# A two-layer hybrid network on one core: the last four slabs by token tile, single accumulator banks, and cross attention's loads in steps

## The chip, the core and the metric

The kernel runs on one core of a Trainium2 chip. The metric is the device time of one execution in microseconds. An engine here is one of TensorE (PE; its weight loads are PEld), VectorE (DVE), ScalarE (ACT), GpSimd (POOL) and SyncE (SP, which issues most of the DMAs).

## The reference

256 tokens of width 2048 go through two layers. Each layer adds to the residual stream h, in this order, a mixer, a cross attention over 256 memory rows, and a feed-forward network with a convolution of width 3:

```
for l in range(DEPTH):
    hn = _rmsnorm(h, norm_mix[l])
    h = h + (_mixer_ab if l % 2 == 0 else _mixer_c)(hn, ...)
    h = h + _cross_attn(_rmsnorm(h, norm_cross[l]), mem_n, w_q_x[l], w_kv_x[l], w_o_x[l])
    h = h + _conv_ffn(_rmsnorm(h, norm_ffn[l]), w_up[l], conv_w[l], conv_b[l], w_down[l])
return _rmsnorm(h, norm_final)
```

The first mixer holds eight heads of block attention and eight of compressed, selected and window attention; the second is a retention. Cross attention has four heads of 128. All is float32, and the weights (525 MB read) are used once.

## The kernel before

Every float32 product is made of three products of rounded parts: a value is split into a high part and a low rest, and high by high, high by low and low by high are summed. `weights` (L224) loads a raw weight tile of 512 KB through SP's queue into one of four buffers; ScalarE rounds it into a high tile (L231), VectorE subtracts for the low one (L232). There are two product forms. `product_b` (L257) gives features by tokens: the weight stands still and 512 columns move (both parts of 256 tokens, L271), then 256 columns (L276). `product_a` (L294) gives tokens by features: a slab of 128 inputs is held for one of two token tiles t of 128, and three matmuls (L304 to L306) run over up to 512 weight columns. A product's accumulator (`acc_tile`, L98) is one PSUM tile of two banks, of which there are two; four more single banks serve everything else.

The order of TensorE's work is written by hand. Side work (the sums of a row norm, heads of attention, the compression of keys and values, turning the residual into the next input) sits in generators in a queue, and `pump(n)` takes n steps of them between product steps. The order on ScalarE, VectorE, GpSimd and SP is a scheduler's, except in the first part.

The start: while the first product runs, rows of x are loaded for the norm's sums (`load_rows`), squared on ScalarE with a running sum (L147), and turned into 1/rms by small VectorE operations (L152 to L185). The first `product_a` after that has weight columns from 4864; its eviction multiplies by the 1/rms.

Cross attention (L528 to L582): the q products of two blocks of columns run interleaved; memory slabs come in four loads of four slabs into raw tiles (`mem_part`, L501) among the q weights; then k and v, then a head's softmax and its product with v (L570), which needs v as evicted by L577.

The feed-forward network (L850 to L897) works in chunks of hidden slabs of 128: 6, 6, 8, 8, 8, 8. While one chunk is computed upward, the one before goes downward in `out_product` (L591), four groups g of 512 columns, each followed by `residual` (L586), which adds the accumulator to h. In the last layer the last downward product is followed per g and t by a square with sum (L147) and a multiplication by the gain (L1047); at the end `norm.column` makes both tiles' 1/rms with Newton steps on VectorE, and scalings (L1055 on VectorE, L1057 on ScalarE) and eight output DMAs (L1058) close the kernel.

Of the kernel before, what the change touches and what calls it, by code (L numbers as in the profile page):

```python
# [20 lines left out]
P = 128  # L21
S = 256
# [7 lines left out]
FFN_CHUNKS = (6, 6, 8, 8, 8, 8)  # L30
# [45 lines left out]
def hybrid_kernel(ctx: ExitStack, tc: tile.TileContext, a, out):  # L76
# [21 lines left out]
    def acc_tile():  # L98
        count[0] += 1
        return ps.tile([P, 2, 512], F32, name=f"acc{count[0]}", tag="acc", bufs=2)  # L100
# [156 lines left out]
    def product_b_steps(ws, xs, evac, step=4, n=None, turn=True):  # L257
# [4 lines left out]
        for i, k0 in enumerate(range(0, n, step)):  # L262
# [6 lines left out]
            def upper(order, end):  # L269
                for k, j in order:  # L270
                    pe.matmul(acc[:, j, :], parts[k - k0][0][:, j * P : (j + 1) * P], xs[k], start=(k == 0),  # L271
                              stop=(end and k == n - 1))

            def lower(order, end):
                for k, j in order:
                    pe.matmul(acc[:, j, 0:S], parts[k - k0][1][:, j * P : (j + 1) * P], xs[k][:, 0:S], start=False,  # L276
# [10 lines left out]
        for j in range(2):  # L287
            evac(j, acc[:, j, :])
# [5 lines left out]
    def product_a_steps(w, xs, c0, ncol, evac, s0=0, ws=None, n=None):  # L294
# [3 lines left out]
        for k in range(n):  # L298
            hi, lo = next(ws)
            for t in range(2):  # L300
                o = acc[:, t, 0:ncol]
                xh = xs[k][:, t * P : (t + 1) * P]
                xl = xs[k][:, S + t * P : S + (t + 1) * P]
                pe.matmul(o, xh, hi, start=(k == 0), stop=False)  # L304
                pe.matmul(o, xh, lo, start=False, stop=False)  # L305
                pe.matmul(o, xl, hi, start=False, stop=(k == n - 1))  # L306
            if k % 2 and k < n - 1:
                yield
        for t in range(2):
            evac(t, acc[:, t, 0:ncol])  # L310
# [55 lines left out]
    with tc.manual_schedule(engines=engines):  # L366
        act.activation(new([P, 1]), eps, AF.Copy, scale=eps)
        load_par(nc.sync, "mix")
        for p in range(ND // 2):
# [14 lines left out]
            if p in (4, 6):  # L384
                for g in range(2):
                    load_rows(p // 2 - 2, g)
# [141 lines left out]
    def cross(l, xs, norm, head_done):  # L528
# [19 lines left out]
        run(*[product_b_steps(weights(w_q, 0, ND, 2 * P * blk, 2 * P), xs, ev_q) for blk in range(2)], n=4)  # L548
# [7 lines left out]
        def head(h):  # L556
# [39 lines left out]
    def mixer_ab(xs, row, col, kcv):  # L596
# [548 lines left out]
```

## Time and profile before

| quantity | us |
|---|---|
| median of 3 runs | 2854.06 (2853.86 to 2856.67) |
| the profiled execution's own time | 2853.46 |
| its span | 2851.70 |
| TensorE busy | 2818.40 |
| VectorE busy | 1923.39 |
| ScalarE busy | 1461.83 |
| first matmul starts | 6.01 |
| last matmul starts | 2836.77 |

The profile is of one execution; the span is the time from its first to its last recorded event, and the execution's own time is 1.76 us longer. The order of groups in the page is by cost; a wait is put down to the instruction that released it last.

### The profile page before, as it was taken

To read this page: it belongs to the slowest core of one execution; us is meant where nothing else is said; L and a number is where in the kernel's file an instruction comes from. 1 tells how busy PE (TensorE), PEld (TensorE's weight loads), DVE (VectorE), ACT (ScalarE), POOL (GpSimd) and SP (SyncE) were. 2 spreads that over 40 slices of the span, in tenths; PEclk is the share of its full clock that TensorE was granted. 3 is DMA by queue.
4 is the path that set the end of the run, shared out by engine and by line. 5 is a ranking of instruction groups with operands and counts; after the bars stand their busy time and mean duration, and the time that the engine had idled before them with its cause. 6 is when DMAs were issued, how large, how long until landed. Compare 5 with 4: busy or idle time off the path is not lost.

```text
span 2851.7 us, 39531 instructions
## 1 busy us (share of the span) xinstructions
PE 2818.4 (99%) x14726; PEld 2404.8 (84%) x14726; DVE 1923.4 (67%) x3139; ACT 1461.8 (51%) x2184; POOL 29.8 (1%) x211
## 2 busy tenths in 40 slices
PE   8999999999999999999999999999999999999997
PEld 7888888888888888888888888888888888888886
DVE  7766776776777677665555555565767776767675
ACT  5444455654555555454444444444565555545453
POOL 0000000000000000000000000000000000000000
PEclk9999999999999999999999999999999999999999
DMA  8534565555555555555555555555545555555554
GB/s 306 168 121 138 173 211 192 173 187 191 188 192 192 189 192 203 192 184 177 177 178 184 187 180 185 180 192 187 195 165 192 192 188 189 190 191 190 190 192 140
DMA packets 149392, 530.11 MB, mean 186 GB/s; under 512 B 16912, under 2 KB 17328, under 8 KB 149200
## 3 DMA queue, kind: packets, MB, share of 16 engines
q1 hardware_dynamic: 147600, 523.65, 53.4%
q0 software_dynamic: 1024, 2.90, 0.3%
q8 instruction: 115, 1.88, 0.3%
q10 hardware_dynamic: 576, 1.05, 0.1%
q14 instruction: 77, 0.63, 0.1%
HBM read 525.43 MB, written 2.10 MB: 185 GB/s over the span
## 4 chain that ended last, share of the span: by engine, by line
PE 96%; ACT 1%; DMA 1%; DVE 1%; issue 0%; SPq 0%; ACTq 0%; DVEq 0%
PE acc L271 32%; PE acc L276 16%; PE acc L304 15%; PE acc L306 14%; PE acc L305 14%; PE bank L338 1%; DMA t<-in_w_in_ab_dram 1%; PE bank L958 0%; ACT t L196 0%; PE bank L474 0%; PE bank L494 0%; PE bank L486 0%; DVE t L232 0%; DMA t<-in_w_kv_x_dram 0%; ACT t L231 0%
## 5 line engine op out<-in xcount | busy, mean ns | idle before, releaser
L232 DVE TENSOR_TENSOR t<-t,t 128x1024 fp32r<-128x1024 f32 x962 | 1174.0, 1221 | 586.4 <-ACT t L231 577.7
L231 ACT ACTIVATE t<-t 128x1024 fp32r<-128x1024 f32 x962 | 1016.2, 1057 | 897.7 <-PE acc L306 548.1
L271 PE MATMUL acc<-t,t 128*128 128x512 f32 x4096 | 992.6, 392 | 10.0 <-DVE t L199 6.0
L271 PEld LDWEIGHTS acc<-t,t 128*128 128x128 f32 x4096 | 750.6, 189 | 155.9 <-DVE t L199 6.0
L304 PE MATMUL acc<-t,t 128*128 128x512 f32 (+2 forms) x1856 | 725.9, 391 | 5.6 <-DVE t L184 5.6
L306 PE MATMUL acc<-t,t 128*128 128x512 f32 (+2 forms) x1856 | 717.3, 386 | 0.0
L305 PE MATMUL acc<-t,t 128*128 128x512 f32 (+2 forms) x1856 | 716.8, 386 | 0.0
L276 PEld LDWEIGHTS acc<-t,t 128*128 128x128 f32 x4096 | 528.5, 191 | 22.1 <-DVE t L632 0.2
L276 PE MATMUL acc<-t,t 128*128 128x256 f32 x4096 | 540.0, 283 | 0.0
L304 PEld LDWEIGHTS acc<-t,t 128*128 128x128 f32 x1856 | 349.6, 188 | 77.7 <-issue 8.7
L306 PEld LDWEIGHTS acc<-t,t 128*128 128x128 f32 x1856 | 349.4, 188 | 70.6
L305 PEld LDWEIGHTS acc<-t,t 128*128 128x128 f32 x1856 | 349.8, 188 | 70.2 <-issue 1.9
L858 ACT ACTIVATE t<-acc 128x256 f32<-128x256 f32 x176 | 65.9, 374 | 222.2 <-PE acc L271 222.2
L861 DVE TENSOR_TENSOR t<-acc,t 128x256 f32<-128x256 f32 x176 | 74.2, 421 | 148.6 <-ACT t L858 148.6
L864 ACT ACTIVATE t<-t,t 128x256 f32<-128x256 f32 x176 | 106.0, 602 | 34.6 <-DVE t L862 34.1
L586 DVE TENSOR_TENSOR t<-t,acc 128x512 f32<-128x512 f32 x152 | 97.7, 684 | 31.0 <-PE acc L306 30.5
L866 DVE SCALAR_TENSOR_TENSOR t<-t,t,t 128x256 f32<-128x256 f32 x176 | 84.6, 481 | 3.1
L865 DVE SCALAR_TENSOR_TENSOR t<-t,t,t 128x256 f32<-128x256 f32 x176 | 84.2, 479 | 0.6 <-ACT t L864 0.6
L862 DVE TENSOR_TENSOR t<-t,t 128x256 f32<-128x256 f32 x176 | 74.5, 423 | 3.0
L314 ACT ACTIVATE t<-acc 128x256 f32<-128x256 f32 x80 | 30.4, 381 | 83.9 <-PE acc L271 81.1
L316 DVE TENSOR_TENSOR t<-acc,t 128x256 f32<-128x256 f32 x80 | 33.4, 418 | 52.5 <-ACT t L314 52.4
L878 ACT ACTIVATE t<-t 128x256 f32<-128x256 f32 x88 | 36.1, 410 | 24.8 <-DVE t L866 24.7
(188 smaller groups left out, 1045.3 us busy)
## 6 DMA issues: line engine op xcount, KB each, us to landing
t<-in_w_up_dram SPq DMA_DIRECT2D x352, 512.0 KB, 3.3
t<-in_w_in_c_dram SPq DMA_DIRECT2D x192, 512.0 KB, 3.3
t<-in_w_down_dram SPq DMA_DIRECT2D x176, 512.0 KB, 3.3
t<-in_w_in_ab_dram SPq DMA_DIRECT2D x80, 512.0 KB, 4.2
t<-in_w_out_c_dram SPq DMA_DIRECT2D x64, 512.0 KB, 3.3
t<-in_w_out_ab_dram SPq DMA_DIRECT2D x32, 512.0 KB, 4.0
t<-in_w_kv_x_dram SPq DMA_DIRECT2D x32, 512.0 KB, 4.3
t<-in_w_q_x_dram SPq DMA_DIRECT2D x16, 512.0 KB, 3.4
```

Source lines behind the costliest of these rows:

```text
L231: act.activation(hi[:, 0 : m * ncol], raw[:, 0 : m * ncol], AF.Copy)
L232: dve.tensor_sub(lo[:, 0 : m * ncol], raw[:, 0 : m * ncol], hi[:, 0 : m * ncol].bitcast(F32))
L271: pe.matmul(acc[:, j, :], parts[k - k0][0][:, j * P : (j + 1) * P], xs[k], start=(k == 0), stop=(end and k == n - 1))
L276: pe.matmul(acc[:, j, 0:S], parts[k - k0][1][:, j * P : (j + 1) * P], xs[k][:, 0:S], start=False, stop=(end and k == n - 1))
L304: pe.matmul(o, xh, hi, start=(k == 0), stop=False)
L305: pe.matmul(o, xh, lo, start=False, stop=False)
L306: pe.matmul(o, xl, hi, start=False, stop=(k == n - 1))
L586: dve.tensor_add(part(t, g), part(t, g), acc)
L862: dve.tensor_mul(u[:, 2:], t, norm.r)
L864: act.activation(c, u[:, 2:], AF.Identity, bias=cp[:, 3, j : j + 1], scale=cp[:, 2, j : j + 1])
L865: dve.scalar_tensor_tensor(c, u[:, 1 : S + 1], cp[:, 1, j : j + 1], c, op0=ALU.mult, op1=ALU.add)
L866: dve.scalar_tensor_tensor(c, u[:, 0:S], cp[:, 0, j : j + 1], c, op0=ALU.mult, op1=ALU.add)
```

## The change

Five parts. (1) An accumulator is a list of two tiles of one bank, of which there are four in all; `product_a` does its last two slabs for token tile 0, evicts it, and then for tile 1. (2) At the start the rows are loaded one per side step, with their square two steps later; the eviction of the product at 4864 does not scale, and VectorE scales later; the compression waits eight steps before its first loads. (3) Cross attention's two q products run one after the other; the memory comes in eight loads of two slabs into tiles of the `long` pool, over ten side steps, and a head's product with v yields between its two halves of keys. (4) The chunks of the second layer are 8, 8, 8, 8, 8, 4. (5) Its last downward product, of four slabs, is `finish`: all four g for token tile 0, then all four for tile 1; the weights of g 0 and 1 are split into input slab buffers, those of 2 and 3 into weight buffers; each tile's 1/rms is made from ScalarE's square root, a reciprocal and one Newton step, and the tile is scaled, half on VectorE and half on ScalarE, and sent. The host's layout of w_down no longer follows the chunks; its parts of two slabs stay the same.

```diff
     def acc_tile():
-        count[0] += 1
-        return ps.tile([P, 2, 512], F32, name=f"acc{count[0]}", tag="acc", bufs=2)
+        count[0] += 2
+        return [ps.tile([P, 512], F32, name=f"acc{count[0] + i}", tag="acc", bufs=4) for i in range(2)]
...
+        for k in range(0, n - 2, 2):
+            for i in range(2):
+                hi, lo = next(ws)
+                for t in range(2):
+                    slab(k + i, t, hi, lo)
+            yield
+
+        parts = [next(ws), next(ws)]
         for t in range(2):
-            evac(t, acc[:, t, 0:ncol])
+            for i in range(2):
+                slab(n - 2 + i, t, *parts[i])
+            evac(t, acc[t][:, 0:ncol])
...
         def mem_steps():
-            for i in range(4):
-                m = mem_part(i)
-                for s in range(4):
-                    xm.append(xhat(m[:, s * S : (s + 1) * S], gain("mem")[:, 4 * i + s : 4 * i + s + 1]))
+            ms = []
+            for p in range(10):
+                if p < 8:
+                    ms.append(long())
+                    nc.sync.dma_start(ms[p], a["mem"][:, 2 * p * S : (2 * p + 2) * S])
+                if p > 1:
+                    for s in (2 * p - 4, 2 * p - 3):
+                        xm.append(xhat(ms[p - 2][:, s % 2 * S : (s % 2 + 1) * S], gain("mem")[:, s : s + 1]))
                 yield
 
         side.extend((norm.row_steps(), mem_steps()))
-        run(*[product_b_steps(weights(w_q, 0, ND, 2 * P * blk, 2 * P), xs, ev_q) for blk in range(2)], n=4)
+        for blk in range(2):
+            run(product_b_steps(weights(w_q, 0, ND, 2 * P * blk, 2 * P), xs, ev_q), n=4)
+        while len(xm) < ND:
+            pump(4)
...
                 pe.matmul(o[:, 0:S], vs[kb][:, h * P : (h + 1) * P], pt[:, kb * S : (kb + 1) * S], start=(kb == 0), stop=(kb == 1))
+                if kb == 0:
+                    yield
...
             norm = Norm()
-            for g in range(4):
-                if g > 1:
-                    for t in range(2):
-                        load_rows(t, g)
-            for g in range(4):
-                for t in range(2):
-                    norm.add(t, g)
-                yield
+            tg = [(t, g) for g in range(4) for t in range(2)]
+            for i in range(10):
+                if i < 8:
+                    load_rows(*tg[i])
+                if i > 1:
+                    norm.add(*tg[i - 2])
+                if i < 9:
+                    yield
...
-        product_a(w, xs, 4864, 256, lambda t, acc: act.activation(vs[:, t, :], acc, AF.Copy, scale=col[:, t : t + 1]))
+        product_a(w, xs, 4864, 256, lambda t, acc: act.activation(vs[:, t, :], acc, AF.Copy))
...
+        def finish(w, xs, s0):
...
+            for g in range(4):
+                for k in (0, 2):
+                    raw = raw_tile()
+                    nc.sync.dma_start(raw, w.part(s0 + k, 2, 512 * g, 512))
...
+            act.activation(small(1), eps, AF.Sqrt)
...
             for t in range(2):
+                ys = []
+                for g in range(4):
+                    o = outs[t][g]
+                    for k in range(4):
+                        hi, lo = ws[g, k]
+                        xh, xl = xs[k][:, t * P : (t + 1) * P], xs[k][:, S + t * P : S + (t + 1) * P]
+                        pe.matmul(o, xh, hi, start=(k == 0), stop=False)
+                        pe.matmul(o, xh, lo, start=False, stop=False)
+                        pe.matmul(o, xl, hi, start=False, stop=(k == 3))
+                    residual(g)(t, o)
+                    norm.add(t, g)
+                    y = new([P, 512], F32, "xs", 32)
+                    dve.tensor_mul(y, part(t, g), gains[g])
+                    ys.append(y)
...
+                dve.tensor_scalar(v, norm.sq[:, 4 * t + 3 : 4 * t + 4], 1.0 / D, m, op0=ALU.mult, op1=ALU.add)
+                act.activation(c, v, AF.Sqrt)
+                dve.reciprocal(c, c)
+                dve.tensor_scalar_mul(v, v, -0.5)
+                dve.tensor_mul(q, c, c)
+                dve.tensor_mul(q, q, v)
+                dve.scalar_tensor_tensor(c, q, 1.5, c, op0=ALU.add, op1=ALU.mult)
+                for g, y in enumerate(ys):
+                    if g % 2:
+                        act.activation(y, y, AF.Copy, scale=c)
+                    else:
+                        dve.tensor_scalar_mul(y, y, c)
+                    (act if g % 2 else nc.sync).dma_start(out[0, t * P : (t + 1) * P, g * 512 : (g + 1) * 512], y)
```

ScalarE at the start of the kernel before, up to the evictions of the last product ahead of the columns from 4864 (its accumulators are acc_111 and acc_120; L147 squares rows, L231 converts a weight, L314 evicts):

```order
L147 ACTIVATE t_416,t_409<-t_74 128x512
L147 ACTIVATE t_436,t_409<-t_73 128x512
L147 ACTIVATE t_438,t_409<-t_74 128x512
L231 ACTIVATE t_392<-t_391 128x1024
L147 ACTIVATE t_459,t_409<-t_73 128x512
L147 ACTIVATE t_461,t_409<-t_74 128x512
L147 ACTIVATE t_477,t_409<-t_73 128x512
L147 ACTIVATE t_479,t_409<-t_74 128x512
L231 ACTIVATE t_442<-t_441 128x1024
L314 ACTIVATE t_348<-acc_111 128x256
L314 ACTIVATE t_352<-acc_111 128x256
L314 ACTIVATE t_364<-acc_120 128x256
```

The same place after the change (L148 squares, L232 converts, L322 evicts; the accumulators are single banks, acc_111 and acc_112 of the first feature block and acc_121 of the next):

```order
L148 ACTIVATE t_464,t_408<-t_74 128x512
L148 ACTIVATE t_485,t_408<-t_73 128x512
L232 ACTIVATE t_391<-t_390 128x1024
L148 ACTIVATE t_500,t_408<-t_74 128x512
L232 ACTIVATE t_431<-t_430 128x1024
L148 ACTIVATE t_521,t_408<-t_73 128x512
L148 ACTIVATE t_538,t_408<-t_74 128x512
L322 ACTIVATE t_346<-acc_111 128x256
L322 ACTIVATE t_350<-acc_112 128x256
L232 ACTIVATE t_467<-t_466 128x1024
L322 ACTIVATE t_362<-acc_121 128x256
```

Two squares less and the same two conversions stand ahead of the first eviction, and the conversion that stood behind the first three evictions stands behind two.

SP's DMA issues before, at the first cross attention's q weights (L230 loads a weight, L501 memory slabs):

```order
L230 DMA t_4202<-in_w_out_ab_dram 128x1024
L230 DMA t_4228<-in_w_q_x_dram 128x1024
L501 DMA t_4272<-in_mem_dram 128x1024
L230 DMA t_4287<-in_w_q_x_dram 128x1024
L501 DMA t_4333<-in_mem_dram 128x1024
L230 DMA t_4347<-in_w_q_x_dram 128x1024
L501 DMA t_4373<-in_mem_dram 128x1024
L230 DMA t_4387<-in_w_q_x_dram 128x1024
```

After the change the memory loads (L551) stand earlier, the last of them among the weights of the mixer's output product:

```order
L231 DMA t_3693<-in_w_out_ab_dram 128x1024
L231 DMA t_3711<-in_w_out_ab_dram 128x1024
L551 DMA t_4551<-in_mem_dram 128x512
L231 DMA t_3729<-in_w_out_ab_dram 128x1024
L231 DMA t_3747<-in_w_out_ab_dram 128x1024
```

The q weights themselves, after the change:

```order
L231 DMA t_4228<-in_w_out_ab_dram 128x1024
L231 DMA t_4255<-in_w_q_x_dram 128x1024
L231 DMA t_4301<-in_w_q_x_dram 128x1024
L231 DMA t_4349<-in_w_q_x_dram 128x1024
L231 DMA t_4383<-in_w_q_x_dram 128x1024
L231 DMA t_4427<-in_w_q_x_dram 128x1024
```

The loads of memory have moved ahead of weights that are used before the cross attention, and the q weights follow one another.

ScalarE at the end before (L147 squares, L1057 scales, the outputs' DMAs):

```order
L147 ACTIVATE t_25852,t_19136<-t_73 128x512
L147 ACTIVATE t_25856,t_19136<-t_74 128x512
L147 ACTIVATE t_25935,t_19136<-t_73 128x512
L147 ACTIVATE t_25939,t_19136<-t_74 128x512
L1057 ACTIVATE t_25692<-t_25692,t_25949 128x512
L1057 ACTIVATE t_25775<-t_25775,t_25949 128x512
L1058 DMA out_dram<-t_25692 128x512
L1058 DMA out_dram<-t_25775 128x512
L1057 ACTIVATE t_25858<-t_25858,t_25949 128x512
L1057 ACTIVATE t_25941<-t_25941,t_25949 128x512
L1058 DMA out_dram<-t_25858 128x512
L1058 DMA out_dram<-t_25941 128x512
```

And after (L1113 is the square root with its table load, L1121 scales; the second half is token tile 1):

```order
L1113 ACT_TABLE_LOAD
L1113 ACTIVATE t_26141<-t_26140 128x1
L148 ACTIVATE t_26171,t_19312<-t_74 128x512
L1121 ACTIVATE t_26101<-t_26101,t_26141 128x512
L1121 ACTIVATE t_26138<-t_26138,t_26141 128x512
L1124 DMA out_dram<-t_26101 128x512
L1124 DMA out_dram<-t_26138 128x512
L148 ACTIVATE t_26188,t_19312<-t_74 128x512
L148 ACTIVATE t_26205,t_19312<-t_74 128x512
L148 ACTIVATE t_26225,t_19312<-t_74 128x512
L1113 ACTIVATE t_26230<-t_26229 128x1
L1121 ACTIVATE t_26190<-t_26190,t_26230 128x512
```

The first tile's root, scalings and outputs now stand between the squares of the two tiles.

## Rows read from the trace of the kernel before

**Rows 1.** The page of the kernel before: its first line, the busy time of each engine (share of the span, instructions), and the shares by engine of the chain of work that ended last.

```profile
span 2851.7 us, 39531 instructions
PE 2818.4 (99%) x14726; PEld 2404.8 (84%) x14726; DVE 1923.4 (67%) x3139; ACT 1461.8 (51%) x2184; POOL 29.8 (1%) x211
...
PE 96%; ACT 1%; DMA 1%; DVE 1%; issue 0%; SPq 0%; ACTq 0%; DVEq 0%
```

**Rows 2.** The waits of TensorE over the whole span: waiting line, releaser, then us in total, times, the longest.

```profile
PE acc L271 <- DVE t L199: 6.0, 1, 6.0
PE acc L304 <- DVE t L184: 5.6, 1, 5.6
PE acc L271 <- DVE t L316: 2.1, 2, 1.2
PE acc L271 <- ACT t L231: 1.9, 2, 1.0
PE bank L570 <- ACT t L577: 1.6, 2, 0.8
```

**Rows 3.** Busy time in two stretches (from:to, length, then busy us and instructions of each engine, TensorE's granted clock, DMA share, GB/s).

```profile
530.00:1980.00 1450.00, 1450.00 (x7314) 1230.86 (x7313) 945.70 (x1401) 720.60 (x986) 14.52 (x94) 1.00 0.54 187
2120.00:2837.00 717.00, 717.00 (x3804) 620.18 (x3803) 510.01 (x748) 376.86 (x533) 8.23 (x83) 1.00 0.54 186
```

**Rows 4.** The timeline of TensorE's wait near the start (start us, us, engine, line, operation; a group of several has its whole time; in brackets the idle time before it and its releaser).

```profile
29.27 1.09 PE L271 MATMUL acc<-t,t 128*128 128x512 f32 x4
...
31.18 0.61 ACT L147 ACTIVATE t<-t 128x512 f32<-128x512 f32 x1
...
31.79 1.04 ACT L231 ACTIVATE t<-t 128x1024 fp32r<-128x1024 f32 x1
31.92 0.16 DVE L152 TENSOR_REDUCE t<-t 128x2 f32<-128x8 f32 x1 [1.22 <-ACT t L147]
...
32.74 0.36 ACT L314 ACTIVATE t<-acc 128x256 f32<-128x256 f32 x1
...
34.53 0.42 DVE L316 TENSOR_TENSOR t<-acc,t 128x256 f32<-128x256 f32 x1
...
35.40 0.42 DVE L316 TENSOR_TENSOR t<-acc,t 128x256 f32<-128x256 f32 x1
...
35.97 0.55 PE L304 MATMUL acc<-t,t 128*128 128x256 f32 x1 [5.61 <-DVE t L184]
```

**Rows 5.** Busy time in stretches there and at one of the short waits, columns as in rows 3 (the last three are granted clock, DMA share, GB/s).

```profile
33.00:34.00 1.00, 0.00 (x0) 0.00 (x0) 0.93 (x4) 0.10 (x1) 0.00 (x0) 0.78 1.04 399
34.00:40.00 6.00, 4.03 (x19) 4.06 (x20) 5.47 (x17) 2.82 (x5) 0.00 (x0) 0.50 1.04 394
...
444.00:446.20 2.20, 1.34 (x6) 1.17 (x7) 2.13 (x6) 1.71 (x3) 0.00 (x0) 1.00 0.86 281
```

**Rows 6.** Two successive matmuls of TensorE's timeline behind 41 us.

```profile
41.81 0.28 PE L306 MATMUL acc<-t,t 128*128 128x256 f32 x1
41.93 0.28 PE L304 MATMUL acc<-t,t 128*128 128x256 f32 x1
```

**Rows 7.** The timeline before the probabilities' product of the first cross attention.

```profile
495.07 1.26 ACT L577 ACTIVATE t<-acc,t 128x512 f32<-128x512 f32 x2 [1.66 <-PE acc L306]
...
495.81 1.49 PE L570 MATMUL bank<-t,t 128*128 128x256 f32 x5 [0.78 <-ACT t L577]
```

**Rows 8.** The timeline of the end, from the last matmuls (0.39 us each, started 0.23 apart).

```profile
2836.54 0.39 PE L305 MATMUL acc<-t,t 128*128 128x512 f32 x1
...
2836.77 0.39 PE L306 MATMUL acc<-t,t 128*128 128x512 f32 x1
2837.20 1.28 DVE L586 TENSOR_TENSOR t<-t,acc 128x512 f32<-128x512 f32 x2 [7.25 <-PE acc L306]
2837.92 0.63 ACT L147 ACTIVATE t<-t 128x512 f32<-128x512 f32 x1 [9.32 <-DVE t L586]
...
2838.45 0.19 ACT L147 ACTIVATION_READ_ACCUMULATOR t<-t 128x1 f32 x1
...
2839.60 0.15 DVE L152 TENSOR_REDUCE t<-t 128x2 f32<-128x8 f32 x1
...
2841.97 0.16 DVE L185 SCALAR_TENSOR_TENSOR t<-t,t 128x2 f32<-128x2 f32 x1
...
2843.94 1.33 ACT L1057 ACTIVATE t<-t,t 128x512 f32<-128x512 f32 x2 [0.44 <-ACT t L1057]
```

**Rows 9.** Of the page: the conversion of a weight on VectorE and on ScalarE (busy us, mean ns of one, idle before), and the weights' DMAs of mixer_ab's output product (count, KB each, median us from issue to landing).

```profile
L232 DVE TENSOR_TENSOR t<-t,t 128x1024 fp32r<-128x1024 f32 x962 | 1174.0, 1221 | 586.4 <-ACT t L231 577.7
L231 ACT ACTIVATE t<-t 128x1024 fp32r<-128x1024 f32 x962 | 1016.2, 1057 | 897.7 <-PE acc L306 548.1
...
t<-in_w_out_ab_dram SPq DMA_DIRECT2D x32, 512.0 KB, 4.0
```

**Rows 10.** Busy time in two stretches of the end, columns as in rows 3.

```profile
2843.00:2850.00 7.00, 0.00 (x0) 0.00 (x0) 0.84 (x3) 1.83 (x3) 0.00 (x0) 0.50 0.94 299
...
2850.00:2851.70 1.70, 0.00 (x0) 0.00 (x0) 0.00 (x0) 0.00 (x0) 0.00 (x0) 0.50 0.00 1
```

**Rows 11.** Two groups of ScalarE (line, operation, shapes, count, busy us, mean ns of one, idle before): a table load, and an operation on one column.

```profile
L878 ACT ACT_TABLE_LOAD x2 | 2.6, 1283 | 0.0
...
L367 ACT ACTIVATE t<-t 128x1 f32<-128x1 f32 x1 | 0.3, 294 | 0.0
```

More of the change, by code (lines that the diff above doesn't have):

```diff
@@ L29 @@
 RET_HEADS = 8
-FFN_CHUNKS = (6, 6, 8, 8, 8, 8)
+FFN_CHUNKS = ((6, 6, 8, 8, 8, 8), (8, 8, 8, 8, 8, 4))
 MAGIC = 12582912.0
@@ L270, in upper @@
                 for k, j in order:
-                    pe.matmul(acc[:, j, :], parts[k - k0][0][:, j * P : (j + 1) * P], xs[k], start=(k == 0),
+                    pe.matmul(acc[j], parts[k - k0][0][:, j * P : (j + 1) * P], xs[k], start=(k == 0),
                               stop=(end and k == n - 1))
@@ L275, in lower @@
                 for k, j in order:
-                    pe.matmul(acc[:, j, 0:S], parts[k - k0][1][:, j * P : (j + 1) * P], xs[k][:, 0:S], start=False,
+                    pe.matmul(acc[j][:, 0:S], parts[k - k0][1][:, j * P : (j + 1) * P], xs[k][:, 0:S], start=False,
                               stop=(end and k == n - 1))
@@ L297, in product_a_steps, with slab @@
         acc = acc_tile()
-        for k in range(n):
-            hi, lo = next(ws)
-            for t in range(2):
[L301 to L307, printed above, removed]
-                yield
+        def slab(k, t, hi, lo):
+            o = acc[t][:, 0:ncol]
+            xh, xl = xs[k][:, t * P : (t + 1) * P], xs[k][:, S + t * P : S + (t + 1) * P]
+            pe.matmul(o, xh, hi, start=(k == 0), stop=False)
+            pe.matmul(o, xh, lo, start=False, stop=False)
+            pe.matmul(o, xl, hi, start=False, stop=(k == n - 1))
+        for k in range(0, n - 2, 2):
[5 more added lines that the diff above has]
+        parts = [next(ws), next(ws)]
         for t in range(2):
-            evac(t, acc[:, t, 0:ncol])
+            for i in range(2):
+                slab(n - 2 + i, t, *parts[i])
+            evac(t, acc[t][:, 0:ncol])
     def halves(acc):
@@ L383, in hybrid_kernel @@
                     load_x(x)
-            if p in (4, 6):
-                for g in range(2):
-                    load_rows(p // 2 - 2, g)
             for s in (2 * p, 2 * p + 1):
@@ L615, in start_steps @@
             act.activation(row, on_rows(col), AF.Copy)
+            for t in range(2):
+                dve.tensor_scalar_mul(vs[:, t, :], vs[:, t, :], col[:, t : t + 1])
             for i in range(2):
@@ L639, in compress @@
         def compress(i, kind, t, done):
+            for _ in range(8):
+                yield
             rs = []
@@ L847, in mixer_ab, with ffn @@
         return order, os
-    def ffn(l, xs, norm, done):
+    def ffn(l, xs, norm, done=None, last=None):
         side.append(norm.row_steps())
@@ L890, in ffn @@
         s0, prev = 0, None
-        for n in FFN_CHUNKS:
+        for n in FFN_CHUNKS[l]:
             os = up(s0, n)
@@ L896, in ffn @@
             s0 += n
-        out_product(w_down, prev[1], prev[0], done)
+        if last is None:
+            out_product(w_down, prev[1], prev[0], done)
+        else:
+            last(w_down, prev[1], prev[0])
     def mixer_c(xs, norm, done):
@@ L1060, in hybrid_kernel @@
+        ffn(1, xs_f, n_ffn, last=finish)
     with tc.manual_schedule(engines={mybir.EngineType.PE}):
@@ L1097, in laid_out @@
 def laid_out(name, w):
-    groups = FFN_CHUNKS if name == "w_down" else (w.shape[1] // P,)
     out = []
     for c0, n in WIDTHS[name]:
-        s0 = 0
-        for g in groups:
-            for r0 in range(0, g, 1024 // n):
-                m = min(1024 // n, g - r0)
-                r = (s0 + r0) * P
-                part = w[:, r : r + m * P, c0 : c0 + n].reshape(-1, m, P, n).transpose(0, 2, 1, 3)
-                out.append(part.reshape(-1, m * P * n))
-            s0 += g
+        for r in range(0, w.shape[1], 1024 // n * P):
+            m = min(1024 // n, w.shape[1] // P - r // P)
+            part = w[:, r : r + m * P, c0 : c0 + n].reshape(-1, m, P, n).transpose(0, 2, 1, 3)
+            out.append(part.reshape(-1, m * P * n))
     return np.concatenate(out, axis=1)
```

45 lines of the change are left out of this document (27 added, 18 removed).

## The prediction

> **What bounds the kernel now.** I read the page's busy line and chain first [rows 1]: TensorE is busy 2818.4 of 2851.7 us, and the chain that ended last runs 96% through it. The order of its matmuls is written by hand and their number does not change, so the time can move only through TensorE's 33.3 us without work, through its clock, and through whether new waits arise. The list of its waits comes next [rows 2]: 6.0 before the first matmul, 5.6 in one piece near the start, and 5.6 in three kinds that belong to the two cross attentions (1.9, 2.1, 1.6). These make 17.2; 14.5 follow the last matmul [rows 8, 10], and 1.6 are left for small waits elsewhere. Two long stretches show that nothing else is to be had [rows 3]: from 530 to 1980 and from 2120 to 2837 us TensorE is busy the whole time at granted clock 1.00. So the products, however their weights are cut or cast, cost 0 unless the change makes them wait.
>
> The profiled execution took 2853.46 us, 1.76 more than its span; the median of the runs is 2854.06, 0.60 above it. I add the parts against 2853.46 and then add the 0.60.
>
> **The start.** The timeline of TensorE's long wait [rows 4]: its last matmul group starts at 29.27 and takes 1.09, so it ends at 30.36; the next matmul starts at 35.97. ScalarE meanwhile squares rows (0.61 each, one after the other to 31.79), converts a weight slab (1.04), and only at 32.74 begins to evict the accumulator; VectorE finishes the two halves' adds at 34.95 (34.53 + 0.42) and 35.82. TensorE needs both, since one tile holds both banks. Three edits shorten this. Two accumulators of one bank each: the first matmul waits for the first add alone, 35.82 - 34.95 = 0.87 less. The rows now come one per step, and the order shows five squares ahead of the eviction instead of seven: 2 x 0.61 = 1.22. And the sums of the row norm, a chain of small VectorE operations that begins at 31.92 and reaches into the time of the first add at 34.53, come later, after the eighth square: what their leaving is worth to that add I bound by 0 and 1.3, half of that stretch. So 0.87 + 1.22 = 2.1, and up to 1.3 more: restart between 32.6 and 33.9. Against it, the second bank's add comes 0.87 behind the first, and TensorE has only three matmuls of the first token tile to do meanwhile: 0.36 at full pace, so 0.5 may come back as a second short wait. I take 2.8 gained; bounds 0 (below) and 3.4.
>
> The lower bound comes from the rows: two of the five squares read rows that are issued later than before, in a stretch where the DMA engines are at share 1.04 [rows 5]. If a row lands at 33 rather than 31, the eviction stands behind it on ScalarE, and the wait is as long as before.
>
> Then the clock [rows 5]. It is 0.78 in the slice 33 to 34 and 0.50, the 1.2 GHz level, from 34 to 40, while 19 matmuls of 256 columns take 4.03 us, 0.212 each. At 2.4 GHz, after 41, two of them start 0.12 apart [rows 6]. From 35.97 to 40.4 about 21 run slow: 21 x 0.09 = 1.9. The expected restart falls in the very slice in which the clock falls. I take half, 0.9; bounds 0 and 1.9. In the row of 444 to 446.2 TensorE idled 0.9 and the clock stayed at 1.00; no row has an idle of 2 to 3 us.
> The Trainium skill ("TensorE: Matmul & The Clock Gate", on HAM oscillation) says that short gaps leave the clock alone and longer ones send it to the lower level; both rows agree. By it alone, were the shorter gap short enough, the start would give 1.0 more than I take, and otherwise 0.9 less. Nothing below uses this.
>
> Start: 2.8 + 0.9 = 3.7 gained, bounds 0 and 5.3. The later scaling of the values adds two small VectorE operations; it is beside matmuls, and costs up to 1 only if TensorE comes to wait for the compression there, which now begins eight steps later; I take 0.
>
> **Cross attention, twice.** The waits are 1.9 for the first q weight's conversion, 2.1 for an accumulator before the k and v product, and 1.6 for the values before the probabilities' product [rows 2]. The first stands where the second of two interleaved q products needs its first weight, a few matmuls after the first product did, while ScalarE converts the two one behind the other; one product after the other, that weight is needed 16 matmuls later or more. And q weights follow each other in SP's queue without mem loads between, as the order shows. The second goes because a single bank, not a pair, is awaited. The third: the profile shows ScalarE evicting v from 495.07 (two evictions, 1.26) and TensorE starting 0.78 late at 495.81 [rows 7]. Now the first token tile of v is complete six matmuls before the second, 6 x 0.227 = 1.36, and its eviction of 0.63 fits in that; the second tile's eviction is needed only after the four heads' first key half. So 0.78 goes to 0. 1.9 + 2.1 + 1.6 = 5.6 can go; since the order of ScalarE and VectorE is a scheduler's, I take 5.1, bounds 0 and 5.6.
>
> What the mem loads pass: they now stand among the weights of the mixer before, on SP, and wait for long buffers that TensorE frees. Behind such a load every weight waits. The last (t_4551) awaits a matmul that stands 84 matmuls of 512 columns ahead of the first use of the weight issued next: 84 x 0.227 = 19.1 us, at the pace of the last matmuls [rows 8]. A weight needs 4.0 to land, 1.06 and 1.22 to be converted [rows 9], 6.3, and 8.6 with one other conversion ahead on each engine. 10.5 are left, so I take 0. The squares of mem and the DMA traffic are the same sum as before.
>
> **The end.** The timeline after the last matmul, T = 2837.16 [rows 8]: two residual adds (1.28), squares, a chain of 13 small VectorE operations, 0.195 apart, from the reduction at T + 2.44 to 2842.13; four scalings on ScalarE, the last ending at 2845.27; the last output's data move until 2850 and the span ends 1.70 later [rows 10]. In all 14.5. Afterwards the first token tile has been added, scaled and sent while TensorE does the second one's four products (48 matmuls, 10.9 us). After T there are: one add 0.68; square 0.63 and its read 0.19, ending at T + 1.55; one sum, 0.20; the root, 0.29 by the nearest row, a ScalarE operation of 128 x 1 [rows 11]; five small operations at 0.195, 0.98; so the factor is there at T + 3.1. Then two scalings on ScalarE, 1.33, with two beside them on VectorE: T + 4.4. Issue and landing: before, from 2845.27 to 2850, 4.7, while 2 MB went out at 299 GB/s [rows 10]; now 1 MB. At that rate it takes 3.5 us from the first issue at about T + 3.9, so T + 7.4; with 4.7 behind the last scaling it is T + 9.1. I take T + 7.9, nearer to the rate since half as much stands in line, plus 1.7 to the end of the span: T + 9.6. Gain 4.9, bounds 3.7 and 5.4. A table load for the root costs 1.28 [rows 11]; the order has one at the last slabs' beginning, beside TensorE, and one ahead of the first tile's root, beside the second tile's products, but none between the last squares and the last root. Were it there the gain would be 3.6.
>
> The sixteen input buffers and the conversions of the last weights are ready before TensorE gets there: nothing reads those buffers after the last up product, and the out_product of the chunk before, 192 matmuls or 44 us, lies between. I take 0.
>
> **Sum.** 3.7 + 5.1 + 4.9 = 13.7. 2853.46 - 13.7 = 2839.8, and 0.6 for the median: 2840.4 us. Single banks and the other order of side steps may shift the small waits by 1 either way.
>
> **Rivals.** A: the rows come late on ScalarE at the start. For it: DMA share 1.04 until 40 us, and rows issued one per step between the weights, the last after three more of these. Against it: SP had issued the later squares' rows in time before. Start 0, end 3.7, cross 5.1: 8.8 gained, 2845.3 us. Chance 0.20.
> B: cross attention does not lose its waits, since mem's xhat work is squeezed before the k product, which must wait for all 16 slabs: they are pumped faster, four steps at a time, onto VectorE, which is busy already. For it: all three kinds of wait there end at VectorE or ScalarE [rows 2]. Against: loads are earlier than before. 3.7 + 0 + 4.9: 2845.5 us. Chance 0.10.
> C: the change does not do what it says, at start and in cross alike, since ScalarE and VectorE are ordered by a scheduler: only 3.7 to 4.9 at the end stay, and 1 is lost: about 2850.5, within 0.2%. Chance 0.07.
> D, slower: SP's queue stalls behind a mem load. Nothing else on SP can pass it. It decides from the point where the awaited matmul comes more than 10.5 us later than counted; each us beyond is a us of TensorE, and there are two cross attentions. To be slower than 2859.8 it must eat 13.7 and 5.7 more, so about 9.7 in each, a release 20 us late. TensorE's order excludes that unless the release waits for a reader other than the one that I counted. About 2862; chance 0.03.
> The forecast itself has 0.60, with its own range 2837 to 2844.
>
> **Numbers.** 0.2%, 5.7 us, is about what a measurement of this kernel can tell from no change: faster is below 2848.4, slower above 2859.8. The forecast, A and B are faster: 0.90, less 0.02 for their tails; C and those are same, 0.09; D is slower, 0.03. The range reaches from 2836.5 (all upper bounds: 5.3 + 5.6 + 5.4 = 16.3 gained, 2837.8, and 1 for the small waits) to 2846.5, past A and B; about 0.13 lies outside.
>
> **What would show it.** In the new profile: the wait at about 30 us shorter than 3.5, and clock 1.00 or 0.5 up to 40; no wait of TensorE above 0.3 in either cross attention; 9 to 11 us from the last matmul to the span's end, with the first tile's outputs issued before the last matmul; TensorE's busy sum within 2 us of 2818.4. Wrong would be a TensorE wait for a weight conversion near 310 or 430 us whose load stood behind mem's (D), a square ahead of the first eviction that waited for a DMA (A), waits of the k product on xhat (B), or a table load in the last 5 us.

## The result and the profile after

The changed kernel takes 2838.21 us (median of 4 runs, 2837.16 to 2839.32) against 2853.96 of the kernel before in the same session; ratio 0.9943, 95% interval 0.9931 to 0.9955. That is 15.7 us less; forecast were 13.7. The profiled executions, 2853.46 and 2837.16, differ by 16.3, as do their spans.

The page after, with the line of the chain and TensorE's waits, which answer to [rows 1, 2]:

```profile
span 2835.4 us, 39564 instructions
PE 2815.4 (99%) x14726; PEld 2404.8 (85%) x14726; DVE 1926.7 (68%) x3147; ACT 1483.8 (52%) x2193; POOL 29.9 (1%) x211
...
PE 98%; DMA 1%; DVE 0%; ACT 0%; issue 0%; SPq 0%; ACTq 0%; DVEq 0%
...
PE acc L272 <- DVE t L200: 6.6, 1, 6.6
PE acc L303 <- DVE t L324: 2.6, 1, 2.6
PE bank L723 <- DVE t L716: 1.7, 1, 1.7
```

Three waits are left. Both cross attentions have none. The wait near 30 us has gone from 5.6 to 2.6. The wait of 1.7 is new: it is the compression's second product behind VectorE, from 143 to 145 us. The small waits of the kernel before for L466, the longest of them at 253 us, are gone:

```profile
PE bank L474 <- DVE t L466: 1.3, 3, 0.9
```

The busy time of TensorE fell by 3.0 too, though it has the same 14726 matmuls.

To place the gain I compare the start times of the matmul of the same number in both traces, at places where the order is the same:

| place | before | after | gained so far |
|---|---|---|---|
| first matmul | 6.01 | 6.56 | -0.6 |
| behind the wait near 30 us, clock back at 1.00 | 44.21 | 41.72 | 2.5 |
| before the output product's side work of the first mixer | 373.83 | 370.94 | 2.9 |
| before the first cross attention | 425.24 | 422.27 | 3.0 |
| behind it | 510.44 | 503.62 | 6.8 |
| before the second | 2007.36 | 2000.55 | 6.8 |
| behind it | 2092.86 | 2081.92 | 10.9 |
| last matmul | 2836.77 | 2825.83 | 10.9 |
| end of the span | 2851.70 | 2835.40 | 16.3 |

The start gave 2.5, the stretch from there to 374 us another 0.4, the cross attentions 3.9 and 4.1, the end 5.3, and the long stretches between nothing.

The start in the timeline after, for [rows 4]:

```profile
29.82 0.63 ACT L148 ACTIVATE t<-t 128x512 f32<-128x512 f32 x1 [1.12 <-DMA t<-in_rows_dram]
...
31.74 0.63 ACT L148 ACTIVATE t<-t 128x512 f32<-128x512 f32 x1 [0.25 <-DMA t<-in_rows_dram]
...
32.40 0.63 ACT L148 ACTIVATE t<-t 128x512 f32<-128x512 f32 x1
...
33.03 0.64 ACT L322 ACTIVATE t<-acc 128x256 f32<-128x256 f32 x2
...
33.43 0.76 DVE L324 TENSOR_TENSOR t<-acc,t 128x256 f32<-128x256 f32 x2 [0.68 <-ACT t L322]
...
33.91 0.39 PE L303 MATMUL acc<-t,t 128*128 128x256 f32 x1 [2.55 <-DVE t L324]
```

What the reader is to see: ScalarE sits idle twice, 1.12 and 0.25, because a square's row has not landed, and the evictions that TensorE waits for stand behind these squares. This is what rival A foresaw. And the clock, for [rows 5]:

```profile
33.00:34.00 1.00, 0.09 (x1) 0.10 (x1) 0.57 (x2) 1.00 (x5) 0.00 (x0) 1.00 1.03 388
34.00:40.00 6.00, 6.00 (x38) 6.00 (x39) 4.73 (x12) 4.23 (x9) 0.00 (x0) 0.72 0.93 318
```

It is 1.00 when TensorE restarts at 33.91, and falls all the same, to 0.50 from 35.0 to 38.5: 0.72 on average from 34 to 40.

The end, for [rows 8]:

```profile
2825.83 0.39 PE L1099 MATMUL bank<-t,t 128*128 128x512 f32 x1
2826.26 0.69 DVE L602 TENSOR_TENSOR t<-t,bank 128x512 f32<-128x512 f32 x1 [0.90 <-PE bank L1099]
2826.98 0.63 ACT L148 ACTIVATE t<-t 128x512 f32<-128x512 f32 x1 [2.00 <-DVE t L602]
...
2827.98 0.20 ACT L1113 ACTIVATE t<-t 128x1 f32<-128x1 f32 x1 [0.28 <-DVE t L1112]
...
2828.80 0.16 DVE L1118 SCALAR_TENSOR_TENSOR t<-t,t 128x1 f32<-128x1 f32 x1
2829.00 1.34 ACT L1121 ACTIVATE t<-t,t 128x512 f32<-128x512 f32 x2 [0.81 <-DVE t L1118]
```

From the last matmul's end, 2826.22, to the end of the span are 9.2 us, where there were 14.5; the factor 1/rms is there 2.7 behind it.

### The profile page after: what moved, and what is told of

The parts are those of the page before. It is cut to its first block, busy times and chain, and to the rows that moved or that the text cites. A ratio compares the mean times of both kernels' runs of the same rounds, so it can differ in the third digit from the quotient of the medians.

```text
span 2835.4 us, 39564 instructions
## 1 busy us (share of the span) xinstructions
PE 2815.4 (99%) x14726; PEld 2404.8 (85%) x14726; DVE 1926.7 (68%) x3147; ACT 1483.8 (52%) x2193; POOL 29.9 (1%) x211
## 4 chain that ended last, share of the span: by engine, by line
PE 98%; DMA 1%; DVE 0%; ACT 0%; issue 0%; SPq 0%; ACTq 0%; DVEq 0%
PE acc L272 33%; PE acc L277 17%; PE acc L303 14%; PE acc L305 14%; PE acc L304 14%; PE bank L346 1%; PE bank L981 0%; DMA t<-in_w_in_ab_dram 0%; PE bank L499 0%; PE bank L491 0%; PE bank L479 0%; PE bank L1004 0%; PE bank L574 0%; PE bank L584 0%; PE bank L970 0%; PE bank L983 0%
## 5 line engine op out<-in xcount | busy, mean ns | idle before, releaser
L232 ACT ACTIVATE t<-t 128x1024 fp32r<-128x1024 f32 x954 | 1009.9, 1059 | 952.5 <-PE acc L305 564.2
L303 PE MATMUL acc<-t,t 128*128 128x512 f32 (+2 forms) x1824 | 712.8, 391 | 2.6 <-DVE t L324 2.6
L305 PE MATMUL acc<-t,t 128*128 128x512 f32 (+2 forms) x1824 | 704.7, 386 | 0.0
L304 PE MATMUL acc<-t,t 128*128 128x512 f32 (+2 forms) x1824 | 704.1, 386 | 0.0
L322 ACT ACTIVATE t<-acc 128x256 f32<-128x256 f32 x80 | 30.4, 382 | 67.0 <-PE acc L272 67.0
```

Source lines behind the costliest of these rows:

```text
L232: act.activation(hi[:, 0 : m * ncol], raw[:, 0 : m * ncol], AF.Copy)
```

## The experiments

Each is the changed kernel with one edit, compared with the kernel before in the same session (ratio with its 95% interval); a difference of 0.001 is 2.9 us. The ratios alone don't part neighbours, so the traces decide, by waits and by start times of equal matmuls ("between equal matmuls" below: how much longer one trace takes than the other from one matmul to a later one).

**The cross attention of before.** Edit: `mem_steps` and the q products as before, and no step between the key halves.

```diff
...
-        for blk in range(2):
-            run(product_b_steps(weights(w_q, 0, ND, 2 * P * blk, 2 * P), xs, ev_q), n=4)
-        while len(xm) < ND:
-            pump(4)
+        run(*[product_b_steps(weights(w_q, 0, ND, 2 * P * blk, 2 * P), xs, ev_q) for blk in range(2)], n=4)
...
```

> The changed kernel with the cross attention of before (interleaved q products, memory in raw tiles, no step between a head's two key halves). Theory 1: cross attention gave 8.0 us, as the start times of TensorE's matmuls of equal place in the two traces say: a wait costs its listed idle time, and what the pipeline loses at its two ends as well. Then the time is 2838.2 + 8.0 = 2846.2, and its trace shows waits of some 5.5 there. Rival: cross gave only its listed idle time, 5.5, and the rest of the gain came from elsewhere: 2843.7. A second rival: with single banks and the product by token tiles kept, the second and third kind of wait stay away even with the old cross: 2840 to 2841.

Measured: 2844.07 us (2842.21 to 2845.65), ratio 0.9960 (0.9946 to 0.9975). The waits, besides those of the three kinds above:

```profile
PE acc L272 <- DVE t L324: 2.1, 2, 1.3
...
PE acc L272 <- ACT t L232: 1.0, 1, 1.0
PE bank L575 <- ACT t L582: 0.7, 2, 0.3
PE bank L193 <- DVE t L200: 0.6, 1, 0.6
```

Between equal matmuls the first cross attention costs 5.7 more and the second 1.9, together 7.6, near the theory's 8.0. The wait for an accumulator sums to 2.1 as before, but it stands elsewhere. Before it came once in each cross attention (0.9 and 1.2); now it comes twice in the first, one matmul apart, and not at all in the second:

```profile
442.24 0.49 PE L272 MATMUL acc<-t,t 128*128 128x512 f32 x1 [0.77 <-DVE t L324]
...
444.05 2.81 PE L272 MATMUL acc<-t,t 128*128 128x512 f32 x7 [1.31 <-DVE t L324]
```

Behind these two the clock fell (0.84 from 440 to 447, 0.93 from 447 to 455). So the second rival falls in the first cross attention, where single banks don't keep this wait away; in the second it stayed away, for a reason that no run isolates. The third kind shrank from 1.6 to 0.7, and the wait for a q weight's conversion is left in the second alone.

**Which part of it.** Three runs take the parts singly. First q interleaved again, by the diff above without `mem_steps`:

> The changed kernel with the two q products of cross attention interleaved again; memory loads and head steps stay as changed. Theory: the interleaving made the wait for the first conversion and the wait for the accumulator before the k product, single banks or not; both come back in each layer, 3 to 4 us with what the pipeline loses at their ends: 2841.5. Rival: the memory's raw tiles and xhat work made them: 2838 to 2839, no wait above 0.3 there.

Measured: 2838.43 (2835.55 to 2840.05), ratio 0.9941 (0.9926 to 0.9955); no wait in either cross attention. My theory fell: with the memory loaded as changed, the interleaving costs nothing.

Then the memory as before, with the q products one after the other:

```diff
...
-            for p in range(10):
-                if p < 8:
-                    ms.append(long())
...
+            for i in range(4):
+                m = mem_part(i)
+                for s in range(4):
+                    xm.append(xhat(m[:, s * S : (s + 1) * S], gain("mem")[:, 4 * i + s : 4 * i + s + 1]))
                 yield
```

> The changed kernel with the memory loaded as before, four slabs at a time into weight buffers, with four side steps; q products one after the other, single banks and head steps stay. Theory: this alone made both waits ahead of the k product (conversion and accumulator), so both come back: 1.0 once or twice and 1.0 to 1.3 twice, with what the pipeline loses at their ends 3.5 to 5 in all: 2842.5. Rival: it makes them only together with interleaved q products: 2838 to 2839, and no wait above 0.3 there.

Measured: 2844.86 (2843.25 to 2846.75), ratio 0.9961 (0.9946 to 0.9976). The waits are back at other lines:

```profile
PE acc L277 <- DVE t L233: 2.1, 1, 2.1
...
PE acc L272 <- ACT t L232: 1.5, 1, 1.5
PE bank L193 <- DVE t L200: 1.2, 1, 1.2
```

In the two cross attentions together 5.7 are lost between equal matmuls. SP's issues there, memory (L506) and weights in turn, and ScalarE's conversions of q weights:

```profile
404.82 0.33 SPq L231 DMA_DIRECT2D t<-in_w_q_x_dram  x1
407.12 0.33 SPq L506 DMA_DIRECT2D t<-in_mem_dram  x1
408.82 0.33 SPq L231 DMA_DIRECT2D t<-in_w_q_x_dram  x1
410.69 0.33 SPq L506 DMA_DIRECT2D t<-in_mem_dram  x1
413.41 0.33 SPq L231 DMA_DIRECT2D t<-in_w_q_x_dram  x1
```

```profile
418.01 1.06 ACT L232 ACTIVATE t<-t 128x1024 fp32r<-128x1024 f32 x1 [3.16 <-DMA t<-in_w_q_x_dram]
...
424.17 1.06 ACT L232 ACTIVATE t<-t 128x1024 fp32r<-128x1024 f32 x1 [3.88 <-DMA t<-in_w_q_x_dram]
```

Every second place in the queue goes to memory, and ScalarE is idle 3.2 and 3.9 us until a q weight lands.

Last, the memory in `long` tiles but in four bursts, so that only the loads differ from the run before: their buffers, with these their place in SP's queue, and their size, two slabs instead of four:

> As the run before, but the memory in tiles of the long pool, two slabs each, loaded and multiplied by the gain four slabs at a time in four side steps. Theory 1: the memory in the weights' buffers was the cause, since the q and k weights were loaded later; in long tiles the waits stay away: 2838 to 2839. Theory 2: the burst of 16 slabs' work on ScalarE and VectorE in front of the first conversions was the cause: both waits come back as in the run before.

Measured: 2838.26 (2837.47 to 2839.41), ratio 0.9938 (0.9923 to 0.9953); no wait in either cross attention. SP's issues in the same stretch:

```profile
401.32 17.99 SPq L231 DMA_DIRECT2D t<-in_w_q_x_dram  x7
```

Seven q weights in the time of three. So it is not the burst of 16 slabs' work by itself; the first two kinds of wait come from memory that shares the four weight buffers and the place in SP's queue with the q weights. Buffers, place and size were not tried apart.

**The step between the key halves** taken away (its two lines):

> The changed kernel without the step between a head's two key halves. Theory: the product by token tiles has already taken most of that wait; what comes back is 0.3 in each layer plus 0.26 by which the 16 matmuls themselves took longer: 2839.3. Rival: the wait comes back in full, 0.8 each: 2840.3. Second rival: nothing, 2838.2.

Measured: 2839.02 (2837.67 to 2840.16), ratio 0.9944 (0.9929 to 0.9958). The wait for v is back, 0.7 in two pieces, and each cross attention is 0.6 longer between equal matmuls. The theory holds: that wait was 1.6 before, so 0.9 of it went without the step, which goes with the product by token tiles, and the step took the rest.

**The end of before**, with the chunks 6, 6, 8, 8, 8, 8:

> The changed kernel with the last layer's chunks and the end of before. Theory: the end gave 5.3 us (14.5 against 9.2 from the last matmul to the end of the span), and the smaller last chunk costs TensorE nothing: 2843.5. Rival: the chunks 8, 8, 8, 8, 8, 4 and the last weights cost TensorE something before the last matmul, so that the end gave less in all: 2841 to 2842.

Measured: 2842.62 (2842.49 to 2844.95), ratio 0.9957 (0.9943 to 0.9972). From the last matmul to the end are 13.6, not 14.5, so of the 5.3 the new end gives 4.4; the other 1.0 goes with the product by token tiles, which adds the first tile before TensorE is done (2826.01 to 2826.70, where the last matmul ends at 2827.33). The trace is 1.2 behind the changed kernel at 380 us, by its start, and 1.1 at the last matmul: the smaller last chunk costs nothing, as the theory had it.

**Newton steps instead of the root** at the end, the order by token tile kept:

```diff
...
-                act.activation(c, v, AF.Sqrt)
-                dve.reciprocal(c, c)
...
+                dve.tensor_scalar(i1, v.bitcast(I32), 1, None, op0=ALU.logical_shift_right)
+                dve.tensor_scalar(c, i1, -1.0, 1597463007.0, op0=ALU.mult, op1=ALU.add)
...
```

> The changed kernel with 1/rms of the end by the integer start and three Newton steps on VectorE, as before, instead of ScalarE's root; the order by token tile stays. Theory: of the 5.3 that the end gave, the root gives the difference of the chains: 12 small VectorE operations at 0.195 from the sum on against the root with its crossings (0.48) and five at 0.2: 2.6 to 2.7 against 1.26 on the trace, so 1.3 us slower, 2839.5, and 10.5 from the last matmul to the end of the span. Rival: the outputs' DMAs set the end, so that nothing changes.

Measured: 2839.79 (2839.53 to 2840.53), ratio 0.9942 (0.9926 to 0.9959). 10.3 from the last matmul to the end against 9.2: the root is worth 1.1 (1.3 expected), and the chain of small operations, not the DMAs alone, sets the end.

**The start of before**, single banks kept: row loads in the input loop, all squares two per step, scaled eviction, no waiting compression.

> The changed kernel with the rows, squares, the scaled eviction and the compression's beginning as before; single banks stay. Theory: single banks alone bring 0.9 of the 3.1 by which the wait near 30 us is shorter, the later rows the rest, and the new wait of 1.7 behind the compression goes, so that this part is worth little in all: 2838.2 + 2.2 + 0.4 (clock) - 1.2 = 2839.6, wait near 30 us 4.5 to 4.9. Rival: the later rows are worth the whole 3: 2841.2 with a wait of 5.6.

Measured: 2837.58 (2836.49 to 2837.94), ratio 0.9938 (0.9922 to 0.9955). All of TensorE's waits:

```profile
PE acc L272 <- DVE t L200: 6.6, 1, 6.6
PE acc L303 <- DVE t L324: 4.1, 1, 4.1
```

By 379 us it is 0.7 ahead of the changed kernel: its wait near 30 us is longer by 1.5, and the new wait of 1.7 isn't there. So the moved rows and the later compression are worth nothing together, and single banks, with the order by token tile, gave what was gained up to there. The median is 2 below the theory's 2839.6.

Where they gave it is another matter. This trace has TensorE's order of before up to 420 us, so that the gain over the kernel before can be followed matmul by matmul: 0.6 at 44 us, and 3.0 by 371. The steps between stand at three small waits of before, at 94, 139 and 253 us (0.1, 0.2 and 0.9 as listed), which are gone and give 0.5, 0.7 and 1.2. At the long wait itself TensorE restarts at 35.84, hardly earlier than the 35.97 of before. The wait is listed 1.5 shorter mainly because TensorE reaches it later, at 31.73 against 30.36. ScalarE, with the same order of squares as before, is 0.84 later in this trace (its second square starts at 27.39, before at 26.55):

```profile
27.39 0.62 ACT L148 ACTIVATE t<-t 128x512 f32<-128x512 f32 x1
...
35.84 0.58 PE L303 MATMUL acc<-t,t 128*128 128x256 f32 x1 [4.11 <-DVE t L324]
```

Measured from that square, the restart comes 0.97 earlier.

**Two-bank accumulators.**

```diff
...
-        return [ps.tile([P, 512], F32, name=f"acc{count[0] + i}", tag="acc", bufs=4) for i in range(2)]
+        a = ps.tile([P, 2, 512], F32, name=f"acc{count[0]}", tag="acc", bufs=2)
+        return [a[:, i, :] for i in range(2)]
```

> The changed kernel with accumulators as tiles of two banks again (two of them). Theory: the wait near 30 us grows by 0.4 to 0.9, and in each cross attention a wait for the accumulator before the k product comes back (0.9 to 1.2, each with 0.2 at its ends): 2841.2. Rival: q products one after the other already spread the evictions, so that only the start shows it: 2839.

Measured: 3025.98 (3023.11 to 3026.85), ratio 1.0596 (1.0580 to 1.0612). Neither theory nor rival foresaw it:

```profile
PE acc L304 <- DVE t L603: 126.1, 72, 2.8
PE acc L304 <- ACT t L959: 7.1, 8, 0.9
```

Now the second token tile's matmuls wait in nearly every product for the first tile's eviction, since both are one tile. To see whether that is all, the product's order was undone as well:

> The changed kernel with accumulators of two banks and the product's last two slabs no longer by token tile, both as before (parts 1 and 2 of the code alone are undone, the end's own product keeps its order). Theory: the 188 us that two-bank tiles cost with the product by token tiles are waits of the second tile's matmuls for the first tile's eviction, and vanish here; what is left is 1 to 1.5 more at the start, 0.5 in each cross attention for the values, and 1.7 to 2 at the end where the tiles are shared: 2842. Rival: single banks are worth more than that to every product's beginning: over 2846.

Measured: 2851.74 (2850.49 to 2853.27, 10 runs), ratio 0.9989 (0.9980 to 0.9998). The many waits go, as expected, but it is 10 slower than expected. That is in the rival's range, over 2846, though not every product's beginning costs: near 30 us TensorE waits 4.8, behind the compression 2.4, and in the last products:

```profile
PE acc L1094 <- DVE t L599: 3.7, 2, 2.9
```

The clock falls twice more, behind the wait of 2.4 and behind the one of 2.9. Against the kernel before, its trace has lost 2.3 by 374 us and loses 5.9 in the last products; the cross attentions gain 5.5 and the end 5.3. Without single banks and the order by token tile the rest of the change is worth 0.1%.

**Squares behind the evictions.** To test rival A, the last five squares are held behind the four evictions on ScalarE (`evacs` collects the instructions of `halves`):

```diff
...
-                if i > 1:
+                if i > 4:
+                    with tc.issue_after(evacs[3]):
+                        norm.add(*tg[i - 2])
+                elif i > 1:
                     norm.add(*tg[i - 2])
```

> The changed kernel, with the last five squares of the start's norm held behind the four evictions on ScalarE. Theory: the wait near 30 us (2.55, 3.8 and 3.9 in three traces of kernels that are alike there) is set by squares that wait for their rows' DMA in front of the evictions. Then it becomes 0.8 to 1.9, the same from run to run, and if it is under some 1.3 the clock does not fall behind it: 1.5 to 3.5 us less than the changed kernel, 2835 to 2837. Rival: the weight conversions of ScalarE and VectorE, which also wait for DMAs, set it: the wait stays at 2.5 or more and the time at 2838.

Measured: 2833.97 (2833.54 to 2834.19), ratio 0.9926 (0.9909 to 0.9942); its slowest run is faster than the fastest of the changed kernel. Its wait and its clock:

```profile
32.36 0.38 PE L303 MATMUL acc<-t,t 128*128 128x256 f32 x1 [0.85 <-DVE t L326]
```

```profile
33.00:34.00 1.00, 1.00 (x10) 1.00 (x10) 1.00 (x2) 0.02 (x1) 0.00 (x0) 1.00 1.11 329
34.00:40.00 6.00, 6.00 (x52) 6.00 (x51) 3.14 (x9) 4.27 (x10) 0.00 (x0) 1.00 0.95 347
```

52 matmuls start in the six microseconds in which the changed kernel started 38. The theory holds, and the time is 1 below its range: the wait was set by squares that stood behind their rows' landing, ahead of the evictions, and behind 0.85 the clock stays. Of the 1.7 by which this wait is shorter than the changed kernel's, ScalarE's two idle times there make 1.4; the rest may be the squares' own time. At 44 us this trace is 5.5 ahead of the kernel before, where the changed kernel is 2.5.

**The best of these**: the same, and one more side step ahead of the compression's second product.

> The kernel of the run with five squares behind the evictions, and one more side step between the compression's VectorE work and the product that waited 1.7 us for it. Theory: that wait goes and 1.7 to 1.9 us with it: 2832.2. Rival: the later compressed values make a head wait: 2834 or more.

Measured: 2833.60 (2832.20 to 2834.97), ratio 0.9921 (0.9906 to 0.9936). The wait of 1.7 is gone, one of 0.3 is new at L828, and the last matmul comes 1.8 earlier than in the run before it (1.5 from the first matmul on, which itself starts 0.4 earlier); the medians, 0.4 apart with overlapping runs, don't show it, and only the fastest run comes to the theory's 2832.2.

## Why the prediction was right, point by point

**What bounds it** held in the main: the gain came from TensorE's idle time, and the long stretches gave 0.0. But TensorE's busy sum fell by 3.0, where the prediction named 2 as the limit; 2.0 of it are matmuls stretched by the waits in cross attention (below), and the low clock near the start had stretched others.

**The start**, forecast 3.7, gave 2.5 by 44 us, and that by luck. The wait is listed 3.1 shorter in the profiled execution, against 2.8 forecast, but 1.0 of this is that TensorE reached it later (31.36 against 30.36). In the seven other traces whose kernels have the changed start the wait is 2.9 to 4.3, and the gain at the same matmul is 0.1 to 2.1. The term for two squares less failed: the squares stand behind rows that land late. I had given this, rival A, 0.20; it is the rule in these traces, only milder than priced in most (no gain at all, which two of the seven come near). The term for the single bank, 0.87, held: 0.97 in its own run, measured from ScalarE's squares. The clock term, 0.9, was too large: TensorE works 3.4 us at the lower clock instead of 4.4, worth about 0.4. "I take 0" for the later compression failed by the new wait of 1.7. And the sum left out three small waits, which it had only allowed to shift "by 1 either way": in the run with the start of before their going gave 2.4. If it gave as much here, the new wait took 2.0 of that back, since by 374 us the gain is 2.9.

**Cross attention**, forecast 5.1, measured 8.0. That the waits go was right; the main reasons were not. The interleaving, my first reason for the first wait, is refuted by its own run. "The second goes because a single bank, not a pair, is awaited" did not hold in the first cross attention of the run with the old cross, and was not isolated in the second. The memory's loads, which I named only as a second reason for the first wait, gave most of it: 5.7 of the 8.0. The step between the key halves gave 1.2, and the 1.1 that is left was not parted. The size was off because a listed wait is the idle time between modelled ends. Here is the first of them before:

```profile
430.24 1.30 PE L271 MATMUL acc<-t,t 128*128 128x512 f32 x5
432.51 0.96 PE L271 MATMUL acc<-t,t 128*128 128x512 f32 x3 [0.97 <-ACT t L231]
```

Matmuls start 0.23 apart and last 0.39. The fifth started at 431.54 - 0.39 = 431.15, the next at 432.51: 1.36 apart, so 1.13 are lost where 0.97 is listed. And the three behind it start over 0.96 - 0.39 = 0.57, not 0.46: another 0.11. The run with the q products interleaved has the matmuls of before in the same order without the waits; against it the six waits of the sum cost 7.4 where 5.6 are listed, 0.26 to 0.40 more each, and two of 0.2, for L466, cost 0.5. These make 7.9 of the 8.0.

**The mem loads on SP**, taken as 0, held; rival D showed nothing, and TensorE waited for no weight behind them.

**The end**, forecast 4.9, measured 5.3. The factor came at 2.7 instead of 3.1, since the root took 0.20 and one small operation ran beside another. Scaling, landing and close were within 0.5 of the sum. That 1.0 of it goes with the product by token tiles, and 1.1 with the root, I had not parted.

Rivals B and C did not happen. The total was nearer than its parts: what the start lacked of its forecast, in most traces more than in the profiled one, and what the cross attentions gave beyond theirs partly cancelled.

## What to carry to other kernels

A listed wait of TensorE was less than what it cost here: read the cost from the start of the last instruction before it to the start of the first behind it. Compare two traces by when the engine restarts, too: a wait can be listed shorter only because the engine came to it later. Let transfers that are needed later not share buffers or a place in the queue with the weights that are needed next. When a product is finished tile by tile, give each part that is evicted alone a buffer of its own; one edit of these two without the other can cost more than both bring.

## What the hardware showed unexpectedly

The clock fell after TensorE had gone back to work: in the changed kernel it is still 1.00 when TensorE restarts at 33.91 behind a wait of 2.55, and at 0.50 from 35.0. Over all traces of this case, of TensorE's waits behind its first matmul, no single one of 0.8 to 1.7 us was followed by a fall within 4 us, and every one of 2.36 or more was, or saw the fall while it lasted. In between lie 16 waits, of 1.95 to 2.32, and four of them were followed by a fall. The length alone does not decide it: in the run with two-bank accumulators two waits of 2.03, at the same place of two products, went differently (from the wait's start; the granted clock is the third number from the end, 1.00 and 0.74).

```profile
2563.89:2570.00 6.11, 4.08 (x19) 3.39 (x19) 3.90 (x5) 1.16 (x2) 0.00 (x0) 1.00 0.42 156
2704.63:2711.20 6.57, 4.54 (x14) 3.60 (x14) 3.89 (x5) 1.16 (x2) 0.00 (x0) 0.74 0.44 149
```

Two waits of 0.8 and 1.3 with one matmul between them, in the run with the old cross attention, were also followed by a fall; that is one case. The Trainium skill ("TensorE: Matmul & The Clock Gate", on HAM oscillation) lets short gaps pass and long ones lower the clock; the traces agree at both ends, and what decides near 2 us stays open.
